# ScalarE's copies of the shared products: earlier places in its queue in the hybrid mLSTM / forgetting-attention / conformer layer

## The chip, the cores and the metric

One core of one Trainium2 chip runs the whole layer. The metric is the time of one execution on the device in microseconds (us); the times shown of the kernel before are the median of three runs.

## The reference

One transformer-like layer on 256 tokens of width 2048, followed by a last RMS norm. A wide input projection feeds three mixers (chunkwise mLSTM, forgetting attention, a conformer convolution), their outputs are projected back, and a squared-ReLU feed-forward network closes the layer. The change lies in the feed-forward network, in its second product:

```python
x = x + jnp.concatenate([y_m, y_a, y_c], axis=-1) @ w_out
h2 = rmsnorm(x, norm_ffn)
x = x + jnp.square(jax.nn.relu(h2 @ w_up)) @ w_down     # w_up 2048 x 8192, w_down 8192 x 2048
...
return rmsnorm(x, final_norm)
```

## The kernel before

**Arithmetic.** All matrix products are float32 in effect: each operand is split into a high part (`hi`, rounded to TensorE's fast float32 format) and a low part (`lo`, the rest), and three matmuls add hi·hi, hi·lo and lo·hi into one PSUM bank. Weights come through eight `raw` tiles of 512 KB (SyncE issues the loads, `load`, L351). For every half unit of weights (a step) ScalarE copies `raw` into `hi` (L442, or L410 in a seven-product step) and VectorE subtracts to get `lo` (L463 or L414). There are five `hi` and five `lo` buffers, so the split of step i+5 waits for TensorE to leave step i.

**The feed-forward network** runs in four quarters q = 0 to 3 of 2048 hidden columns. A quarter first makes four up blocks (kind B: 8 steps, four banks each, named f = 0 to 3 here), each squared and split into `hid`. Then `w_down` is applied in two pairs p = 0, 1 of output blocks of 512 columns (kind A: two banks each, one for each half of the tokens). There are four PSUM banks under the tag `mm` and four under `mx`. Tags t0 and t1 change places from quarter to quarter.

**Seven products in place of eight.** In a pair some chunks of four contraction tiles are multiplied by Strassen's scheme in Winograd's form. `SEVEN` gives the order of its seven steps:

```python
SEVEN = (("p3", 0, 1), ("p1", 1, 0), ("p2", 1, 1), ("p5", 1, 0), ("p7", 0, 0), ("p6", 0, 1), ("p4", 1, 1))
```

p2, p3 and p4 belong to one output each and add straight into the pair's own banks. p1, p5, p6 and p7 are shared by several outputs; they get the four banks of the other tag, t1, and must be copied out by ScalarE when the last seven-product chunk has added to them. `add_up` makes these four copies, chained in the order p1, p5, p6, p7 (though TensorE finishes p7 before p6): in q = 0 straight into an accumulator (L1381, tile `acc0`, or `fnb` for p = 1), in later quarters into a tile `zz` (L1386), two copies to a tile, and VectorE adds each tile to the accumulator (L1390). VectorE's four further steps (L1404 to L1417) bring the sums into the result once, after q = 2 for p = 1 and after q = 3 for p = 0 (`fin`). A seven-product step whose weights are sums of weights needs one more VectorE step, `raw<-raw` (L398), ahead of its `hi`. The plain blocks of `w_down` leave their banks by `gather` (ScalarE L1432 into `z`, VectorE L1438 into `x2t`).

**Where the four banks are wanted at once.** In pair p = 1 the units run y0 x0 s1 x3 s2 y3 (s: seven products, x and y: plain chunks of the two outputs). After p4, the last step of s2, TensorE has only y3 left (two steps, 24 matmuls) and then begins the next quarter's first up block, which takes the four t1 banks: f = 0 to 3 each wait for a copy. These are boundary 1 (q = 0 to 1, copies L1381), boundary 2 (q = 1 to 2) and boundary 3 (q = 2 to 3). In q = 3 the pair p = 0 runs x0 y0 x1 s2 y1 s3, and directly after p4 of s3 the plain block of column group 2 begins in the same tag, which takes two of the banks at once: boundary 4. The pairs p = 0 of q = 0 to 2 are followed by seven products of p = 1 only some steps later.

**What sets the order.** The program's text is written out by a planner while the kernel is built. Each engine has a queue of tasks with a cost, predecessors and a priority; when an engine is free by the planner's clock, it takes, of the tasks that are ready by then, the one with the lowest `prio`. `lag` is added to the time at which a task counts as ready. Splits of weights have prio -1, `gather`'s copies -2 with lag 0.3, the copies of shared products -0.8 with lag 1.5:

```python
r = max(r, d.fin + (0.0 if d.eng == t.eng else LAT))
q = room(t.takes)
return None if q is None else max(r + t.lag, q)
...
p = t.prio + (1.5 if t.table and t.table != table[0] else 0.0)
key = (0, p, i, r) if r <= now + 0.02 else (1, r, p, i)
```

On the chip each engine then works its list in that fixed order, and waits at each instruction for its semaphores.

Of the kernel before, what the change touches and what calls it, by code (L numbers as in the profile page):

```python
# [33 lines left out]
def trunk(ctx: ExitStack, tc, x, norm_mix, w_in, b_in, mlstm_conv_w, mlstm_conv_b,  # L34
# [3 lines left out]
    x, w_in, w_out, w_up, w_down, out = x[0], w_in[0], w_out[0], w_up[0], w_down[0], out[0]  # L38
# [9 lines left out]
    def sbt(pl, shape, name, dt=F32, bufs=1, tag=None):  # L48
        return pl.tile(shape, dt, name=name, tag=tag or name, bufs=bufs)
# [38 lines left out]
    def task(*a, **kw):  # L88
        t = Task(*a, **kw)
        queue[t.eng].append(t)  # L90
        return t

    def t_act(cost, fn, *a, **kw):
        return task("act", cost, fn, *a, **kw)

    def t_dve(cost, fn, *a, **kw):
        return task("dve", cost, fn, *a, **kw)

    def t_pe(cost, fn, *a, **kw):
        return task("pe", cost, fn, *a, **kw)  # L100
# [89 lines left out]
    def cd(n):  # L190
        return 0.13 + 0.00105 * n

    def cut(c):
        return slice(c * 512, (c + 1) * 512)
# [11 lines left out]
    def pl(name):  # L206
        return pools[name][1]
# [386 lines left out]
    wb = Buf(mm_rot)  # L594
# [24 lines left out]
    for j in range(2):  # L619
# [9 lines left out]
        for h in range(4):  # L629
            o = xt[j][:, cut(h)]  # L630
# [16 lines left out]
    for c2 in range(KC // 2):  # L647
        b = mx_buf()
        ts = []
# [121 lines left out]
    for i in range(2):  # L771
# [19 lines left out]
        for c in range(2):  # L791
            jg.append(join(lambda c=c, o_g=o_g: o_g(c), bg, c, col("bug", 4 + 2 * i + c),
                           takes=[gbuf] if c == 0 else [], deps=[jg[-1]]))
# [20 lines left out]
    for j in range(2):  # L814
# [16 lines left out]
        p = t_pe(0.45, f1, list(tap.values()), prio=20, takes=[b])  # L831
# [8 lines left out]
    for h in range(2):  # L840
# [22 lines left out]
        p = t_pe(0.45, f1, ln_t, prio=20, takes=[b], uses=[lnx_buf[0]])  # L863
# [3 lines left out]
        for c in range(2):  # L867
# [7 lines left out]
                  prio=-2, uses=[b.bufs[j]]) for j in range(2)]  # L875
# [334 lines left out]
    def seven_of(b0, b1, tag, stat, q):  # L1210
        return dict(b=(b0, b1), tag=tag, hid=stat, q=q,
                    extra={x: Buf(mx_rot if tag == "mx" else mm_rot) for x in SHARED},
                    done={x: Task("pe", 0.0, None) for x in SHARED})
# [114 lines left out]
    for c in range(4):  # L1328
# [6 lines left out]
        for i2 in range(2):  # L1335
# [10 lines left out]
            p = t_pe(0.45, f, ad, prio=-1, takes=[tb])  # L1346
# [23 lines left out]
    def add_up(p, q, o, fin):  # L1370

        ts, both = [late_open], []
        for m, x in enumerate(("p1", "p5", "p6", "p7")):
            if q and m % 2 == 0:
                wb = Buf(zz_rot)

            def f(m=m, x=x):
                if (p, 0) not in acc:
                    acc[p, 0] = sbt(pl("late"), [P, 4, 512], "acc0") if p == 0 else \
                        sbt(pl("late"), [P, D], "fnb").rearrange("p (m n) -> p m n", m=4)  # L1380
                act.activation(acc[p, 0][:, m, :], o["extra"][x].t, AF.Copy)  # L1381

            def f1(m=m, x=x, wb=wb if q else None):
                if m % 2 == 0:
                    wb.t = sbt(pl("late"), [P, 4, S], "zz", bufs=2).rearrange("p (m h) t -> p m (h t)", m=2)
                act.activation(wb.t[:, m % 2, :], o["extra"][x].t, AF.Copy)  # L1386

            def f2(m=m, wb=wb if q else None):
                t = acc[p, 0][:, m - 1:m + 1, :]
                dve.tensor_add(t, t, wb.t)  # L1390

            ts.append(t_act(0.6, f1 if q else f, [o["done"][x]] + ts[-1:], prio=-0.8,
                            takes=[wb] if q and m % 2 == 0 else [], uses=[o["extra"][x]], lag=1.5))
            if q and m % 2:
                both.append(t_dve(1.22, f2, [ts[-1]] + both, prio=-0.6, uses=[wb]))
        ts += both
        if not fin:
            return []

        def g(i):  # L1400
            a1, a5, a6, a7 = (acc[p, 0][:, m, :] for m in range(4))

            def out(j, c, t):
                dve.scalar_tensor_tensor(x2[0][:, j, cut(c)], t, rs2[:, j:j + 1], x2[0][:, j, cut(c)],  # L1404
                                         op0=OP.mult, op1=OP.add)

            if i == 0:
                dve.tensor_add(a6, a6, a1)
                out(0, 2 * p, a1)
            elif i == 1:  # L1410
                dve.tensor_add(a7, a7, a6)
                out(1, 2 * p, a7)
            elif i == 2:
                dve.tensor_add(a6, a6, a5)
                out(0, 2 * p + 1, a6)
            else:
                dve.tensor_add(a5, a5, a7)  # L1417
                out(1, 2 * p + 1, a5)

        gs = [ts[-1]]  # L1420
        for i in range(4):
            gs.append(t_dve(2 * cd(512), lambda i=i: g(i), [gs[-1], rs_t], prio=-0.5))
        return gs[1:]
# [17 lines left out]
    def x2_ap(j, sl):  # L1441
        return lambda: x2[0][:, j, sl]
# [4 lines left out]
    for q in range(4):  # L1447
        t0, t1 = (("mm", "mx"), ("mx", "mm"))[q % 2]
        for c in range(4):
            b = block_units(blk("B", 512, lambda: big["h"], "h", (t0, t1)[c % 2]), w_up, 2048 * q + 512 * c)  # L1450
            zb, wb = Buf(z_rot), Buf(zz_rot)
# [31 lines left out]
        for p in range(2):  # L1483
            sv = GROUPS[q, p]
            if not sv:
                for c in (2, 3):
                    bs[c] = block_units(down(c, t1), w_down, 512 * c, KC * q)
                continue
            b0, b1 = bs[2 * p], bs[2 * p + 1] = down(2 * p, t0), down(2 * p + 1, t0)
            o = seven_of(b0, b1, t1, lambda: big["hid"], "hid%d" % q)  # L1490
            pair_units(b0, b1, w_down, 1024 * p, KC * q, sv, p == 1,
                       lambda c: dict(o=o, sums=lambda: xsum[c], packed=packed(q, c), fourth=own if c == 3 else None))
            got = add_up(p, q, o, q == (3, 2)[p])
            for i, t in enumerate(got):
                shared[2 * p + i // 2, i % 2] = t
            if p == 1 and got:
                fn_t = t_ctl(fn_in, got)
# [22 lines left out]
    for j in range(2):  # L1520
# [8 lines left out]
        for h in range(2):  # L1529
            hs = slice(1536 + h * 256, 1792 + h * 256)  # L1530
            o = x2_ap(j, hs)
# [39 lines left out]
    for i, toks in items:  # L1571
        u, half = steps[i]["u"], steps[i]["h"]
        d = units[u]
        if steps[i]["p"]:
            p, o, g = steps[i]["p"], steps[i]["o"], steps[i]["g"]
# [30 lines left out]
        m = len(d["ks"]) // 2  # L1606
# [68 lines left out]
```

## Time and profile before

| | us |
|---|---|
| median of three runs (1135.47 to 1137.18) | 1135.47 |
| the profiled execution | 1134.14 |
| its span | 1131.7 |
| TensorE busy in the span | 1111.2 (98%) |
| VectorE busy | 874.0 (77%) |
| ScalarE busy | 655.6 (58%) |

The time of the profiled execution is its span and 2.4 us around it. Busy time is a sum over the whole span; where a change in one place counts, the rows of that place say what each engine waited for. A row of the timeline has the start, the duration, the engine, the line, the operation and its tiles (out<-in), the count of instructions merged into it, and in brackets the idle time ahead of it with what ended it. The durations of matmuls are modelled (0.39), while their starts are recorded: in an unbroken stream the starts lie 0.227 apart.

### The profile page before, as it was taken

To read this page: it belongs to the slowest core of one execution; us is meant where nothing else is said; L and a number is where in the kernel's file an instruction comes from. 1 tells how busy PE (TensorE), PEld (TensorE's weight loads), DVE (VectorE), ACT (ScalarE), POOL (GpSimd) and SP (SyncE) were. 2 spreads that over 40 slices of the span, in tenths; PEclk is the share of its full clock that TensorE was granted. 3 is DMA by queue.
4 is the path that set the end of the run, shared out by engine and by line. 5 is a ranking of instruction groups with operands and counts; after the bars stand their busy time and mean duration, and the time that the engine had idled before them with its cause. 6 is when DMAs were issued, how large, how long until landed. Compare 5 with 4: busy or idle time off the path is not lost.

```text
span 1131.7 us, 15579 instructions
## 1 busy us (share of the span) xinstructions
PE 1111.2 (98%) x5812; PEld 950.7 (84%) x5812; DVE 874.0 (77%) x1160; ACT 655.6 (58%) x932; POOL 17.0 (2%) x40
## 2 busy tenths in 40 slices
PE   8999999999999999999999999999999999999996
PEld 7888788888888888888887888887888887888875
DVE  6679998887676786668994677996577999567993
ACT  7445376777775565545664554765454666455662
POOL 1000000010000000000000000000000000000000
PEclk9999999999999999999999999999999999999998
DMA  8866554547555385565756555657644658655452
GB/s 308 254 196 193 185 167 137 181 149 242 168 183 167 121 269 169 154 202 164 228 192 235 168 169 161 232 183 243 190 163 149 225 186 270 225 173 186 160 175 74
DMA packets 130818, 214.97 MB, mean 190 GB/s; under 512 B 6796, under 2 KB 48056, under 8 KB 130360
## 3 DMA queue, kind: packets, MB, share of 16 engines
q1 hardware_dynamic: 130136, 212.93, 58.2%
q10 hardware_dynamic: 608, 1.06, 0.3%
q8 instruction: 45, 0.74, 0.3%
q14 instruction: 29, 0.24, 0.1%
HBM read 211.87 MB, written 2.10 MB: 189 GB/s over the span
## 4 chain that ended last, share of the span: by engine, by line
PE 94%; DMA 2%; ACT 1%; issue 1%; DVE 1%; POOLq 0%; POOL 0%; ACTq 0%; DVEq 0%
PE mm L57 64%; PE mx L57 30%; DMA raw<-in_w_in_dram 1%; DMA x<-in_x_dram 1%; ACT hi L442 0%; DMA rowp<-in_norm_mix_dram 0%; ACT z L1432 0%; ACT zz L1386 0%; PE mx L1343 0%; PE mx L989 0%; DMA rowp<-in_norm_ffn_dram 0%; DVE lo L414 0%; DVE lo L463 0%; ACT x2t L1548 0%; PE mx L1022 0%
## 5 line engine op out<-in xcount | busy, mean ns | idle before, releaser
L463 DVE TENSOR_TENSOR lo<-raw,hi 128x1024 fp32r<-128x1024 f32 x332 | 397.7, 1223 | 192.6 <-issue 129.3
L442 ACT ACTIVATE hi<-raw 128x1024 fp32r<-128x1024 f32 x332 | 346.5, 1057 | 263.9 <-PE mm L57 166.7
L410 ACT ACTIVATE hi<-raw 128x1024 fp32r<-128x1024 f32 x105 | 111.5, 1062 | 93.2 <-PE mm L57 34.9
L57 PE MATMUL mm<-hi,hid 128*128 128x512 f32 x488 | 155.3, 389 | 2.2 <-ACT zz L1386 2.2
L57 PE MATMUL mm<-x,hi 128*128 128x512 f32 x640 | 156.4, 394 | 0.0
L414 DVE TENSOR_TENSOR lo<-raw,hi 128x1024 fp32r<-128x1024 f32 x105 | 126.5, 1223 | 13.1 <-ACT hi L410 12.5
L57 PEld LDWEIGHTS mm<-x,hi 128*128 128x128 f32 x640 | 116.9, 188 | 23.1 <-ACT tmp L564 0.4
L57 PE MATMUL mx<-h,hi 128*128 128x512 f32 x512 | 123.0, 391 | 3.9 <-ACT fnb L1381 2.3
L57 PE MATMUL mm<-h,hi 128*128 128x512 f32 x512 | 123.2, 391 | 1.7 <-ACT zz L1386 1.5
L57 PEld LDWEIGHTS mx<-h,hi 128*128 128x128 f32 x512 | 94.1, 188 | 23.3 <-ACT fnb L1381 3.1
L57 PEld LDWEIGHTS mm<-h,hi 128*128 128x128 f32 x512 | 94.0, 188 | 21.0 <-ACT zz L1386 2.0
L57 PEld LDWEIGHTS mm<-hi,hid 128*128 128x128 f32 x488 | 91.6, 188 | 21.6 <-ACT zz L1386 2.7
L57 PE MATMUL mx<-hi,hid 128*128 128x512 f32 x304 | 98.5, 389 | 0.0
L57 PE MATMUL mm<-lo,hid 128*128 128x512 f32 x244 | 95.1, 390 | 0.1
L57 PEld LDWEIGHTS mm<-x,lo 128*128 128x128 f32 x640 | 82.0, 191 | 3.2
L57 PE MATMUL mm<-x,lo 128*128 128x256 f32 x640 | 83.0, 282 | 0.0
L398 DVE TENSOR_TENSOR raw<-raw 128x1024 f32<-128x1024 f32 x60 | 73.3, 1222 | 0.7
L57 PE MATMUL mm<-hi,y 128*128 128x512 f32 x232 | 73.5, 392 | 0.0
L57 PEld LDWEIGHTS mm<-h,lo 128*128 128x128 f32 x512 | 65.6, 191 | 2.5
L57 PEld LDWEIGHTS mx<-h,lo 128*128 128x128 f32 x512 | 65.7, 191 | 2.5
L57 PEld LDWEIGHTS mx<-hi,hid 128*128 128x128 f32 x304 | 57.1, 188 | 11.8
L57 PE MATMUL mm<-h,lo 128*128 128x256 f32 x512 | 66.4, 283 | 0.0
(244 smaller groups left out, 1289.5 us busy)
## 6 DMA issues: line engine op xcount, KB each, us to landing
raw<-in_w_up_dram SPq DMA_DIRECT2D x128, 512.0 KB, 3.8
raw<-in_w_down_dram SPq DMA_DIRECT2D x128, 512.0 KB, 5.1
raw<-in_w_in_dram SPq DMA_DIRECT2D x92, 512.0 KB, 3.5
raw<-in_w_out_dram SPq DMA_DIRECT2D x32, 512.0 KB, 4.6
raw<-in_w_in_dram SPq DMA_DIRECT2D x8, 516.0 KB, 3.4
raw<-in_w_in_dram SPq DMA_DIRECT2D x4, 544.0 KB
x<-in_x_dram SPq DMA_DIRECT2D x8, 256.0 KB, 4.2
x2t<-in_x_dram SPq DMA_DIRECT2D x2, 1024.0 KB
```

What stands on the lines that cost most here:

```text
L57: pe.matmul(o, l, r, start=start, stop=stop, skip_group_check=True)
L398: sums[i] = t_dve(C_LO, lambda: dve.tensor_sub(piece(*o), piece(*l), piece(*r)), after + [arrival(*l), arrival(*r)], prio=-1)
L410: act.activation(hl[i][0], piece(u, h), AF.Copy)
L414: dve.tensor_sub(hl[i][1], piece(u, h), hl[i][0].bitcast(F32))
L442: act.activation(hl[i][0], raws[u, h][0], AF.Copy)
L463: dve.tensor_sub(hl[i][1], raws[u, h][0], hl[i][0].bitcast(F32))
```

## The change

`add_up` gets a flag `soon`, true for p = 1 in every quarter and for the pair that is closed (`fin`). Where it is true the copies of shared products get prio -2 in place of -0.8 and lag 0.3 in place of 1.5. Elsewhere nothing changes.

```diff
     def add_up(p, q, o, fin):
 
         ts, both = [late_open], []
+        soon = p == 1 or fin
         for m, x in enumerate(("p1", "p5", "p6", "p7")):
...
-            ts.append(t_act(0.6, f1 if q else f, [o["done"][x]] + ts[-1:], prio=-0.8,
-                            takes=[wb] if q and m % 2 == 0 else [], uses=[o["extra"][x]], lag=1.5))
+            ts.append(t_act(0.6, f1 if q else f, [o["done"][x]] + ts[-1:], prio=-2 if soon else -0.8,
+                            takes=[wb] if q and m % 2 == 0 else [], uses=[o["extra"][x]], lag=0.3 if soon else 1.5))
```

No instruction is added or removed; TensorE's order is the same. The lists of ScalarE and VectorE change around the four boundaries. Lines behind the new one have numbers higher by one.

ScalarE at boundary 1, before, from the copy of p1 (the L1381 are p1, p5, p6, p7; L410 is the high part of p4; the first two L442 those of y3, then the next up block's):

```order
L1381 ACTIVATE fnb<-mx 128x512
L1432 ACTIVATE z<-mm,st 128x512
L410 ACTIVATE hi<-raw 128x1024
L442 ACTIVATE hi<-raw 128x1024 x4
L1432 ACTIVATE z<-mm,st 128x512
L442 ACTIVATE hi<-raw 128x1024 x2
L1381 ACTIVATE fnb<-mx 128x512
L442 ACTIVATE hi<-raw 128x1024
L1432 ACTIVATE z<-mm,st 128x512
L1381 ACTIVATE fnb<-mx 128x512
L1432 ACTIVATE z<-mm,st 128x512
L1381 ACTIVATE fnb<-mx 128x512
```

and now:

```order
L1382 ACTIVATE fnb<-mx 128x512
L1433 ACTIVATE z<-mm,st 128x512
L1382 ACTIVATE fnb<-mx 128x512
L410 ACTIVATE hi<-raw 128x1024
L442 ACTIVATE hi<-raw 128x1024
L1382 ACTIVATE fnb<-mx 128x512
L442 ACTIVATE hi<-raw 128x1024
L1382 ACTIVATE fnb<-mx 128x512
L1433 ACTIVATE z<-mm,st 128x512
L442 ACTIVATE hi<-raw 128x1024 x5
```

The copy of p5 stands ahead of p4's high part, that of p6 behind y3's first high part and that of p7 behind its second; before, three of them stood behind seven or more high parts.

ScalarE at boundary 2, before, from the copy of p1 (the L1386 are p1, p5, p6, p7); boundary 3 reads the same with `mm` and `mx` exchanged:

```order
L1386 ACTIVATE zz<-mm 128x512
L1432 ACTIVATE z<-mx,st 128x512
L1386 ACTIVATE zz<-mm 128x512
L410 ACTIVATE hi<-raw 128x1024
L442 ACTIVATE hi<-raw 128x1024 x4
L1432 ACTIVATE z<-mx,st 128x512
L442 ACTIVATE hi<-raw 128x1024 x2
L1386 ACTIVATE zz<-mm 128x512
L442 ACTIVATE hi<-raw 128x1024
L1432 ACTIVATE z<-mx,st 128x512
L1386 ACTIVATE zz<-mm 128x512
```

and now:

```order
L1387 ACTIVATE zz<-mm 128x512
L1433 ACTIVATE z<-mx,st 128x512
L1387 ACTIVATE zz<-mm 128x512
L410 ACTIVATE hi<-raw 128x1024
L1387 ACTIVATE zz<-mm 128x512
L442 ACTIVATE hi<-raw 128x1024
L1387 ACTIVATE zz<-mm 128x512
L442 ACTIVATE hi<-raw 128x1024
L1433 ACTIVATE z<-mx,st 128x512
L442 ACTIVATE hi<-raw 128x1024 x5
L1433 ACTIVATE z<-mx,st 128x512
```

The copies of p1 and p5 keep their places. The copy of p6 now stands ahead of both high parts of y3, and that of p7 between them.

VectorE at boundary 2, before, from the add of p1 and p5 (L1390; L414 is the low part of p4, then come y3's two and the next block's):

```order
L1390 TENSOR_TENSOR fnb<-fnb,zz 128x1024
L414 TENSOR_TENSOR lo<-raw,hi 128x1024
L463 TENSOR_TENSOR lo<-raw,hi 128x1024 x6
L1438 TENSOR_TENSOR x2t<-x2t,z 128x2x512
L463 TENSOR_TENSOR lo<-raw,hi 128x1024
L1390 TENSOR_TENSOR fnb<-fnb,zz 128x1024
L1438 TENSOR_TENSOR x2t<-x2t,z 128x2x512
```

and now:

```order
L1391 TENSOR_TENSOR fnb<-fnb,zz 128x1024
L414 TENSOR_TENSOR lo<-raw,hi 128x1024
L463 TENSOR_TENSOR lo<-raw,hi 128x1024
L1391 TENSOR_TENSOR fnb<-fnb,zz 128x1024
L463 TENSOR_TENSOR lo<-raw,hi 128x1024 x6
L1439 TENSOR_TENSOR x2t<-x2t,z 128x2x512 x2
```

The add of p6 and p7 has moved from the end of this piece to between the two low parts of y3.

ScalarE at boundary 4, before, around the copy of p1 (the first L1386; L410 is the high part of p4, the L442 are those of the plain block that follows):

```order
L1432 ACTIVATE z<-mx,st 128x512
L1386 ACTIVATE zz<-mm 128x512
L1432 ACTIVATE z<-mx,st 128x512
L410 ACTIVATE hi<-raw 128x1024
L442 ACTIVATE hi<-raw 128x1024 x4
L1432 ACTIVATE z<-mx,st 128x512
L442 ACTIVATE hi<-raw 128x1024
L1386 ACTIVATE zz<-mm 128x512 x2
L442 ACTIVATE hi<-raw 128x1024
L1386 ACTIVATE zz<-mm 128x512
```

and now:

```order
L1387 ACTIVATE zz<-mm 128x512
L1433 ACTIVATE z<-mx,st 128x512 x2
L1387 ACTIVATE zz<-mm 128x512
L410 ACTIVATE hi<-raw 128x1024
L442 ACTIVATE hi<-raw 128x1024
L1387 ACTIVATE zz<-mm 128x512
L442 ACTIVATE hi<-raw 128x1024
L1387 ACTIVATE zz<-mm 128x512
L442 ACTIVATE hi<-raw 128x1024 x2
L1433 ACTIVATE z<-mx,st 128x512
```

The copy of p5 stands ahead of p4's high part, those of p6 and p7 behind the first and second high part of the block that follows.

VectorE at boundary 4, before, from the sum of weights (L398) that p4 needs:

```order
L398 TENSOR_TENSOR raw<-raw 128x1024
L1438 TENSOR_TENSOR x2t<-x2t,z 128x2x512
L414 TENSOR_TENSOR lo<-raw,hi 128x1024
L463 TENSOR_TENSOR lo<-raw,hi 128x1024 x5
L1438 TENSOR_TENSOR x2t<-x2t,z 128x2x512
L1390 TENSOR_TENSOR acc_5417<-acc_5417,zz 128x1024
```

and now:

```order
L398 TENSOR_TENSOR raw<-raw 128x1024
L1439 TENSOR_TENSOR x2t<-x2t,z 128x2x512
L1391 TENSOR_TENSOR acc_5417<-acc_5417,zz 128x1024
L414 TENSOR_TENSOR lo<-raw,hi 128x1024
L463 TENSOR_TENSOR lo<-raw,hi 128x1024 x6
L1439 TENSOR_TENSOR x2t<-x2t,z 128x2x512
```

The add of p1 and p5 into the accumulator now stands ahead of p4's low part (L414).

## Rows read from the trace of the kernel before

**Rows 1.** The page's first part: busy us, share of the span, instructions.

```profile
PE 1111.2 (98%) x5812; PEld 950.7 (84%) x5812; DVE 874.0 (77%) x1160; ACT 655.6 (58%) x932; POOL 17.0 (2%) x40
```

**Rows 2.** TensorE's waits, 429 to 1120 us: total us, times, longest.

```profile
PE mm L57 <- ACT zz L1386: 3.8, 2, 2.2
PE mx L57 <- ACT fnb L1381: 2.3, 2, 1.8
PE mx L57 <- ACT zz L1386: 1.5, 1, 1.5
```

**Rows 3.** The timeline around boundary 1.

```profile
588.13 0.39 PE L57 MATMUL mx<-hi,xsums 128*128 128x512 f32 x1
...
588.29 1.06 ACT L410 ACTIVATE hi<-raw 128x1024 fp32r<-128x1024 f32 x1 [0.40 <-DVE raw L398]
...
589.38 1.23 DVE L414 TENSOR_TENSOR lo<-raw,hi 128x1024 fp32r<-128x1024 f32 x1 [1.19 <-ACT hi L410]
...
591.08 0.39 PE L57 MATMUL mm<-hi,hid 128*128 128x512 f32 x1
...
597.88 0.61 PE L57 MATMUL mx<-h,hi 128*128 128x512 f32 x2
...
600.65 0.61 ACT L1381 ACTIVATE fnb<-mx 128x512 f32<-128x512 f32 x1
...
601.31 3.28 PE L57 MATMUL mx<-h,hi 128*128 128x512 f32 x13 [0.56 <-ACT fnb L1381]
```

**Rows 4.** The timeline around boundary 2.

```profile
761.73 0.39 PE L57 MATMUL mm<-hi,xsums 128*128 128x512 f32 x1
...
762.15 0.60 ACT L1386 ACTIVATE zz<-mm 128x512 f32<-128x512 f32 x1 [0.67 <-PE mm L57]
...
762.67 1.06 ACT L410 ACTIVATE hi<-raw 128x1024 fp32r<-128x1024 f32 x1
...
763.64 3.89 ACT L442 ACTIVATE hi<-raw 128x1024 fp32r<-128x1024 f32 x4
...
764.45 0.39 PE L57 MATMUL mm<-hi,xsums 128*128 128x512 f32 x1
...
765.06 6.90 DVE L463 TENSOR_TENSOR lo<-raw,hi 128x1024 fp32r<-128x1024 f32 x6
...
766.24 0.62 PE L57 MATMUL mx<-hi,hid 128*128 128x512 f32 x2
766.70 0.39 PE L57 MATMUL mx<-lo,hid 128*128 128x512 f32 x1
...
771.91 0.84 PE L57 MATMUL mm<-h,hi 128*128 128x512 f32 x3
...
773.65 0.59 ACT L1386 ACTIVATE zz<-mm 128x512 f32<-128x512 f32 x1
...
774.29 1.89 PE L57 MATMUL mm<-h,hi 128*128 128x512 f32 x7 [1.53 <-ACT zz L1386]
```

**Rows 5.** The timeline around boundary 4.

```profile
1072.27 0.39 PE L57 MATMUL mm<-hi,xsums 128*128 128x512 f32 x1
...
1072.57 1.22 DVE L1438 TENSOR_TENSOR x2t<-x2t,z 128x1024 f32<-128x1024 f32 x1
...
1073.84 1.23 DVE L414 TENSOR_TENSOR lo<-raw,hi 128x1024 fp32r<-128x1024 f32 x1
...
1075.22 0.39 PE L57 MATMUL mx<-hi,hid 128*128 128x512 f32 x1
...
1077.03 0.39 PE L57 MATMUL mm<-hi,hid 128*128 128x512 f32 x1
...
1079.02 1.07 ACT L1386 ACTIVATE zz<-mm 128x512 f32<-128x512 f32 x2
1079.65 0.50 PE L57 MATMUL mm<-hi,hid 128*128 128x512 f32 x1 [2.23 <-ACT zz L1386]
```

**Rows 6.** ScalarE's longest sum of waits, 429 to 1120 us, same columns.

```profile
ACT hi L442 <- PE mm L57: 85.8, 56, 2.7
```

## The prediction

> **What bounds the kernel.** I read the busy times first: TensorE 98%, VectorE 77%, ScalarE 58% of the span [rows 1]. So time is to be won only where TensorE stands still, and I read its list of waits over the feed-forward network next. It holds three lines with five waits, 7.6 us together, and all end with a copy of a shared product [rows 2]; no transfer and no weight split stands in it. Then I read the timeline around each boundary, since idle time there is counted from modelled ends; I count from starts, of which an unbroken stream has one every 0.227 us.
>
> At boundary 1 the new block starts its bank 0 and bank 1 at 597.88, could start bank 3 at 597.88 + 3 x 0.227 = 598.56, and starts it at 601.31, behind the copy of p7 at 600.65 [rows 3]: 2.75 us lost. At boundary 2 bank 0 starts at 771.91, bank 3 could at 772.59 and does at 774.29, again behind p7's copy at 773.65 [rows 4]: 1.70 us. Boundary 3 has the same order and shows the same idle time (1.5 us in both, the mx line and the rest of the mm line [rows 2]): 1.70 us. At boundary 4 the second bank could start at 1077.03 + 0.23 = 1077.26 and does at 1079.65, behind the copies at 1079.02 [rows 5]: 2.39 us. Together **8.54 us**, which is all that there is to win.
>
> **The waits that go.** In the new lists all four copies stand ahead of at most one or two weight splits of what follows p4. At boundary 2 p7's copy can run at about 766.4 (worked out below) where bank 3 is wanted at 772.6; at boundary 1 at about 592.8, wanted at 598.6; at boundary 4 p5's copy at 1072.7, wanted at 1077.3. So I take all of the 8.54 us as removed. No instruction is added, so nothing else is charged but the places: what stands behind a copy that waits.
>
> **The waits that come.** ScalarE's new list has copies that wait for TensorE, and behind them stand the high parts, behind those VectorE's low parts, and for these TensorE waits. Some durations: a copy starts 0.42 after the start of the product's last matmul (761.73 to 762.15), the next instruction 0.52 later (762.67), a high part takes 1.06, a low part 1.23 with one every 1.15 (6.90 for six), both read off boundary 2 [rows 4].
>
> *Boundaries 2 and 3.* p6's last matmul starts at 764.45, so its copy cannot start before 764.87. ScalarE is free at 763.64, when before it began y3's first high part [rows 4]. It now idles 1.23, copies, and begins that high part at 765.39, ready at 766.45; VectorE's low part follows from 766.49 and is ready for TensorE, with 0.04 for the signal, at 767.75. TensorE wants the high part at 766.47 and the low part, its second matmul, at 766.70 [rows 4]. The high part is just in time, the low part 1.05 late. Next comes p7's copy (766.36), y3's second high part (766.9 to 767.9), VectorE's add of p6 and p7 (767.6 to 768.9) and the second low part, 768.8 to 770.0; TensorE, now 1.05 later, wants it near 770.5: just in time, by 0.5. Net at each of the two: 1.70 - 1.05 = **0.65**.
>
> *Boundary 1.* Here the copy of p5 has moved ahead of p4's high part. p5's last matmul starts at 588.13, its copy at 588.55, the high part at 589.07 in place of 588.29: 0.78 later. The low part then starts at 590.16 in place of 589.38 and is ready at 590.16 + 1.23 + 0.04 = 591.43; TensorE wants it at 591.08 + 0.23 = 591.31 [rows 3]: 0.12 late. y3's first high part now stands ahead of p6's copy and is ready at 591.1; its low part at 592.6, wanted at 592.8. Net 2.75 - 0.12 = **2.63**.
>
> *Boundary 4.* p5's last matmul starts at 1072.27, its copy at 1072.69, p4's high part at 1073.21, ready at 1074.27. But VectorE now adds p1 and p5 between the add at 1072.57 and p4's low part, which therefore moves from 1073.84 by one add to about 1074.85 and is ready at 1076.12; TensorE wants it at 1075.22 + 0.23 = 1075.45 [rows 5]: 0.67 late. The low part behind it is ready at 1077.25, wanted at 1077.6. Net 2.39 - 0.67 = **1.72**.
>
> Sum: 2.63 + 0.65 + 0.65 + 1.72 = 5.65. TensorE works on alone behind every boundary and the last block ends the span, so I take the gain through to the end one for one. VectorE's closing steps behind q = 2 and q = 3 change places with low parts that are made five steps ahead; I cost that at nothing. If that cover were gone, a low part late by one add would cost up to 1.2. The final norm's load moves back by two weight loads in SyncE's queue; it is wanted only near the end of q = 3, and two loads come ahead of it instead of behind: nothing again.
>
> [...] ScalarE idled 0.67 ahead of p5's copy at 762.15 and the high part behind it began only at 762.67, after the copy [rows 4]. [...]
>
> **The sum against the times.** The profiled execution took 1134.14, of which 1131.7 is span; it would take 1134.14 - 5.65 = 1128.5. The median of the three runs is 1.33 above the profiled one, so the forecast for the median is 1135.47 - 5.65 = **1129.8 us**. About 0.2% (2.3 us) is what a measurement of this kernel can tell from no change.
>
> **Bounds of the terms.** What goes is measured; the new waits are worked out from chained durations, and each link can be off by one slot. From below they are nothing: 8.54 gained, 1126.9. From above: at boundary 1 a low part is late by another 1.15, one slot of VectorE, at boundaries 2 and 3 the second low part of y3 is late too (0.5 of margin against one slot of 1.15: 0.65 more each), at boundary 4 one slot more: 1.15 + 0.65 + 0.65 + 1.15 = 3.6 less, that is 2.05 gained, 1133.4. I take the chain as worked out, since each of its links is a distance that this stretch itself shows.
>
> **Rivals.**
>
> *All of it is won: 1126.9.* For it: high parts run up to four in a row ahead of TensorE (763.64, four in 3.89 [rows 4]), and ScalarE's largest sum of waits is high parts that wait for TensorE to leave a buffer, 85.8 us in 56 waits [rows 6], so in most places a high part has time in hand. Against it: just here y3's low part, made from 765.06 to 766.28, has only 0.38 in hand, and the copy of p6 costs its high part 1.75.
>
> *It is given back: about 1134.5, no change that can be told.* The removed idle time of TensorE comes back as waits for splits behind the boundary: buffers come free earlier, and ScalarE and VectorE, which before caught up while TensorE stood, do not. For it: at boundary 2 the add of p6 and p7 has also moved ahead of y3's second low part. Against it: VectorE has 23% and ScalarE 42% of the span free [rows 1], so a lag of 1.4 us is made up in some 6 us of VectorE's time, while the block's low parts are made several steps ahead. With one further low part late by a whole slot at each boundary the gain is 5.65 - 4 x 1.15 = 1.05.
>
> *Slower: about 1140.* One mechanism: the copies at the head of ScalarE's queue hold the high parts, and the lag reaches TensorE in full. Price at its worst, at each boundary: the wait for p6 (1.23), two copies ahead of the high part (2 x 0.52) and one add ahead of the low part (1.15), 3.4 us; four times 13.7 against 8.54 gained, 5.1 slower, 1140.6. It decides where the first low part behind the copies comes later by more than the time in hand and the old wait together: at boundary 2 by more than 0.38 + 1.70 = 2.08 us. I work out a shift of 766.49 - 765.06 = 1.43 there, 0.78 at boundary 1 and 1.0 at boundary 4, all short of that, and at boundary 4 against 0.34 + 2.39. So this needs a wait that I have not seen.
>
> *The change does not do what it says.* It could fail only if the new order were another than written; the lists show the moves at all four boundaries, so I give it nothing of its own.
>
> **How the numbers follow.** Forecast (gain of 4 to 7): 0.71. All won: 0.09. Given back: 0.13, of which a third still gains over 0.2%. Slower: 0.07. Faster by over 0.2%: 0.71 + 0.09 + 0.04 = 0.84; within 0.2%: 0.10; slower by over 0.2%: 0.06, the last rival but for its small end. The range takes the bounds of the terms, 1126.9 and 1133.4, and leaves the given-back and slower cases out, 0.16 to 0.2 together: 1126.9 to 1133.4.
>
> **What would show it.** In the trace after, TensorE's waits on lines of the copies (L1382, L1387) should be gone or under 0.3 us each. In their place there should be a gap of some 1 us ahead of the second matmul of y3 at boundaries 2 and 3, ended by the low part L463, one of 0.1 to 0.2 at boundary 1 and one of 0.6 to 0.7 ahead of p4's second matmul at boundary 4, both ended by L414. ScalarE should idle some 1.2 us ahead of p6's copy at boundaries 2 and 3. Each quarter's first up block should start unbroken over all four banks. If TensorE still waits at bank 3, the copies come later than worked out; if no gap stands ahead of y3, the first rival holds; if gaps turn up two or more steps behind a boundary, the gain is being given back.

## The result and the profile after

| | before | after |
|---|---|---|
| median | 1135.51 us (1135.19 to 1137.18, 6 runs) | 1127.99 us (1127.71 to 1128.21, 6 runs) |
| ratio, 95% interval | | 0.9932 [0.9919, 0.9945] |
| span of the profiled execution | 1131.7 us | 1125.8 us |

The change makes the kernel 0.7% faster, 7.5 us in the median and 5.9 us between the two profiled spans. Both numbers count: over all runs on record, those of before lie in groups, near 1133.8, 1135.5 and 1137 us, and its profiled execution (1134.14) is one of the lowest; runs of after all lie within 0.5 us.

Busy times on the page of after, to set beside [rows 1]:

```profile
PE 1110.5 (99%) x5812; PEld 950.2 (84%) x5812; DVE 873.7 (78%) x1160; ACT 655.8 (58%) x932; POOL 17.0 (2%) x40
```

TensorE's waits of after, 429 to 1120 us (total us, times, longest), against [rows 2]:

```profile
PE mm L57 <- DVE lo L463: 0.8, 1, 0.8
PE mx L57 <- DVE lo L463: 0.8, 1, 0.8
PE mx L57 <- DVE lo L414: 0.5, 1, 0.5
```

All five waits for copies are gone. Three shorter ones for low parts, 2.1 us together, have come: the L463 at boundaries 2 and 3, the L414 at boundary 4.

The timeline of after at boundary 1, against [rows 3]:

```profile
588.41 0.60 ACT L1382 ACTIVATE fnb<-mx 128x512 f32<-128x512 f32 x1 [0.67 <-PE mx L57]
588.90 1.05 ACT L410 ACTIVATE hi<-raw 128x1024 fp32r<-128x1024 f32 x1
...
589.99 1.23 DVE L414 TENSOR_TENSOR lo<-raw,hi 128x1024 fp32r<-128x1024 f32 x1 [1.94 <-ACT hi L410]
...
591.27 0.50 PE L57 MATMUL mm<-lo,hid 128*128 128x512 f32 x1
591.61 0.64 PE L57 MATMUL mm<-hi,hid 128*128 128x512 f32 x2
...
598.01 3.79 PE L57 MATMUL mx<-h,hi 128*128 128x512 f32 x16
```

The copy of p5 (588.41) is first and p4's high part follows. The low part is done so that its matmul starts at 591.27, 0.11 behind the 591.16 that an unbroken stream would have had. The new block's sixteen first matmuls run as one piece from 598.01, over all four banks.

At boundary 2, against [rows 4]:

```profile
762.08 0.60 ACT L1387 ACTIVATE zz<-mm 128x512 f32<-128x512 f32 x1 [1.14 <-PE mm L57]
762.57 1.05 ACT L442 ACTIVATE hi<-raw 128x1024 fp32r<-128x1024 f32 x1
763.45 0.74 PE L57 MATMUL mx<-hi,hid 128*128 128x512 f32 x2
...
763.66 1.22 DVE L463 TENSOR_TENSOR lo<-raw,hi 128x1024 fp32r<-128x1024 f32 x1 [1.30 <-ACT hi L442]
...
764.94 0.50 PE L57 MATMUL mx<-lo,hid 128*128 128x512 f32 x1 [0.75 <-DVE lo L463]
...
770.28 3.79 PE L57 MATMUL mm<-h,hi 128*128 128x512 f32 x16
```

Here the lines show the whole price: ScalarE stands 1.14 us ahead of p6's copy, y3's high part begins only behind it at 762.57, VectorE's low part at 763.66, and the matmul that needs it starts at 764.94 in place of 763.91, 1.03 late. The block behind (770.28) is again unbroken.

At boundary 4, against [rows 5]:

```profile
1069.54 1.22 DVE L1391 TENSOR_TENSOR acc<-acc,zz 128x1024 f32<-128x1024 f32 x1
...
1070.67 1.22 DVE L414 TENSOR_TENSOR lo<-raw,hi 128x1024 fp32r<-128x1024 f32 x1
...
1071.05 0.39 PE L57 MATMUL mx<-hi,hid 128*128 128x512 f32 x1
...
1071.95 0.50 PE L57 MATMUL mx<-lo,hid 128*128 128x512 f32 x1 [0.50 <-DVE lo L414]
```

The add of p1 and p5 stands ahead of p4's low part. Its matmul is wanted at 1071.28 and starts at 1071.95, 0.67 late.

I counted all of TensorE's lateness at the four boundaries in this manner, from one recorded start to the next and against 0.227 us a matmul: before 2.92 + 2.24 + 2.27 + 2.51 = 9.94 us, after 0.23 + 1.55 + 1.55 + 0.79 = 4.12 us. The difference, 5.82, is the 5.9 us between the spans. What it leaves out is the rest of the median's 7.5.

### The profile page after: what moved, and what is told of

Its sections match the earlier page's. It is cut to its first block, busy times and chain, and to the rows that moved or that the text cites. A ratio compares the mean times of both kernels' runs of the same rounds, so it can differ in the third digit from the quotient of the medians.

```text
span 1125.8 us, 15581 instructions
## 1 busy us (share of the span) xinstructions
PE 1110.5 (99%) x5812; PEld 950.2 (84%) x5812; DVE 873.7 (78%) x1160; ACT 655.8 (58%) x932; POOL 17.0 (2%) x40
## 4 chain that ended last, share of the span: by engine, by line
PE 96%; DVE 1%; DMA 1%; issue 1%; ACT 1%; POOLq 0%; POOL 0%; ACTq 0%; DVEq 0%
PE mm L57 65%; PE mx L57 30%; DMA x<-in_x_dram 1%; ACT hi L442 0%; DMA rowp<-in_norm_mix_dram 0%; PE mx L989 0%; PE mx L1343 0%; DVE lo L463 0%; DVE lo L414 0%; PE mx L656 0%; ACT x2t L1549 0%; PE mx L1022 0%; DVE x L642 0%; DVE h L642 0%; DVE x L635 0%
## 5 line engine op out<-in xcount | busy, mean ns | idle before, releaser
L463 DVE TENSOR_TENSOR lo<-raw,hi 128x1024 fp32r<-128x1024 f32 x332 | 397.7, 1222 | 185.9 <-issue 124.4
L442 ACT ACTIVATE hi<-raw 128x1024 fp32r<-128x1024 f32 x332 | 346.7, 1058 | 255.0 <-PE mm L57 160.0
L410 ACT ACTIVATE hi<-raw 128x1024 fp32r<-128x1024 f32 x105 | 111.5, 1062 | 91.9 <-PE mm L57 34.4
L414 DVE TENSOR_TENSOR lo<-raw,hi 128x1024 fp32r<-128x1024 f32 x105 | 126.3, 1221 | 13.8 <-ACT hi L410 12.9
L398 DVE TENSOR_TENSOR raw<-raw 128x1024 f32<-128x1024 f32 x60 | 73.2, 1220 | 0.7
L57 PE MATMUL mx<-h,lo 128*128 128x256 f32 x512 | 66.4, 283 | 0.0
```

What stands on the lines that cost most here:

```text
L57: pe.matmul(o, l, r, start=start, stop=stop, skip_group_check=True)
L398: sums[i] = t_dve(C_LO, lambda: dve.tensor_sub(piece(*o), piece(*l), piece(*r)), after + [arrival(*l), arrival(*r)], prio=-1)
L410: act.activation(hl[i][0], piece(u, h), AF.Copy)
L414: dve.tensor_sub(hl[i][1], piece(u, h), hl[i][0].bitcast(F32))
L442: act.activation(hl[i][0], raws[u, h][0], AF.Copy)
L463: dve.tensor_sub(hl[i][1], raws[u, h][0], hl[i][0].bitcast(F32))
```

## Experiments

The edits are shown against the changed kernel, where nothing else is said.

**The boundaries apart.** Three kernels make the change at one kind of boundary only, and a fourth is the kernel before again, on the same chip.

```diff
-        soon = p == 1 or fin
+        soon = p == 1 and q == 0        # boundary 1 only
```

> The change at boundary 1 alone. Theory of the chain of slots (the prediction's sum): 2.63 us gained, 1132.9 by the median. Rival that all the old wait is won: 2.75. Rival that something besides the four boundaries went (the medians moved by 7.5 us where the sum has 5.65): the part in which it lies gains 1.4 to 1.9 us more than its term; here 4 to 4.5 if it lies at boundary 1.

```diff
-        soon = p == 1 or fin
+        soon = p == 1 and q > 0         # boundaries 2 and 3 only
```

> The change at boundaries 2 and 3 alone. Theory of the chain: 2 x 0.65 = 1.3 us gained, 1134.2, a gap of 1.04 us ahead of the second matmul of y3 at each. All of the old wait won: 3.4 us. Extra beyond the boundaries lying here: 2.7 to 3.2.

```diff
-        soon = p == 1 or fin
+        soon = p == 0 and fin           # boundary 4 only
```

> The change at boundary 4 alone. Theory of the chain: 2.39 - 0.67 = 1.72 us gained, 1133.8. All won: 2.39. Extra lying here: 3.1 to 3.6.

> The kernel before, unchanged, for a second trace of it. If its profiled execution in the first trace was a short one, the span here is 1 to 1.4 us over 1131.7, and the rows show where: at a boundary (then the terms of the sum are larger than the first trace had them) or elsewhere (then the change took it away in passing). If not, the span is 1131.7 and the time 1134.1.

| change at | median, us | lowest | ratio [95%] | gain, medians | gain, lowest runs | term predicted |
|---|---|---|---|---|---|---|
| none (before again) | 1135.55 | 1133.42 | 0.9997 [0.9987, 1.0007] | 0.1 | | |
| boundary 1 | 1132.42 | 1131.12 | 0.997 [0.996, 0.998] | 3.2 | 2.7 | 2.63 |
| boundaries 2 and 3 | 1133.99 | 1132.60 | 0.9986 [0.9977, 0.9995] | 1.7 | 1.2 | 1.30 |
| boundary 4 | 1133.50 | 1132.20 | 0.9975 [0.9966, 0.9985] | 2.2 | 1.6 | 1.72 |

The medians are set against 1135.65 (29 runs of before shared by the four, 1133.80 to 1138.16), the lowest runs against 1133.80. By lowest runs the three gains are near the predicted terms, and together 5.5; a lowest run is known only to some 0.4 us, as before again went down to 1133.42 on the same chip. The starts in the traces are firmer: before less after they give 2.69 at boundary 1, 0.69 and 0.72 at 2 and 3, and 1.72 at 4. By medians the three gains make 7.0, near the whole 7.5. They are 0.4 to 0.6 over the term at every one of the three, where the expectations had looked for the whole extra in one place. So nothing is missing between the boundaries; what is missing is something that the middle run of before has and its lowest does not.

The second trace of before was taken to catch it, but its execution was one of the lowest again (1133.42, span 1131.0), so no trace of before itself shows a longer run. The trace of the kernel with boundary 1 alone does, since its profiled execution (1132.66) was not one of the lowest. Behind boundary 4, which this kernel leaves as it was, TensorE waits 2.2 us for a copy, and then:

```profile
1076.69 0.79 PE L57 MATMUL mm<-hi,hid 128*128 128x512 f32 x1 [2.23 <-ACT zz L1387]
1077.28 0.63 PE L57 MATMUL mm<-lo,hid 128*128 128x512 f32 x1
1077.70 1.05 PE L57 MATMUL mm<-hi,hid 128*128 128x512 f32 x2
1078.56 0.63 PE L57 MATMUL mm<-lo,hid 128*128 128x512 f32 x1
1078.98 1.02 PE L57 MATMUL mm<-hi,hid 128*128 128x512 f32 x2
1079.84 0.39 PE L57 MATMUL mm<-lo,hid 128*128 128x512 f32 x1
```

The starts are 0.42 us apart (1077.28 to 1077.70) where they are 0.227 elsewhere. The windows of the same kernel (stretch; us; for PE, PEld, DVE, ACT and POOL busy us and count; granted clock; DMA share; GB/s):

```profile
1074.00:1076.00 2.00, 0.46 (x3) 0.03 (x1) 2.00 (x3) 2.00 (x3) 0.00 (x0) 1.00 0.97 280
1076.00:1078.00 2.00, 1.31 (x3) 1.12 (x4) 2.00 (x3) 1.12 (x3) 0.00 (x0) 0.60 0.64 166
1078.00:1080.00 2.00, 2.00 (x6) 1.52 (x6) 2.00 (x2) 0.00 (x0) 0.00 (x0) 0.54 0.99 366
1080.00:1082.00 2.00, 2.00 (x11) 1.61 (x10) 0.45 (x2) 1.50 (x2) 0.00 (x0) 1.00 1.03 379
```

Behind the wait the granted clock falls to 0.60 and 0.54, the means of two windows of 2 us, and is back at 1.00 from 1080 on. From 1076.69 to 1079.84 seven matmuls take 3.15 us in place of 7 x 0.227 = 1.59; some 0.1 of that is the first spacing behind the waits at the boundaries, 0.34 at full clock too (below), so the fall costs **about 1.45 us**. The other two kernels, whose boundary 1 is as before, show a clock of 0.83 there in 600 to 610 us, behind the two waits for copies; counted in the same way they lose 1.6 each. The profiled execution of before has 1.00 throughout 600 to 770 and 1060 to 1080. Shown here are the first of the two waits at boundary 1 in the trace of before (the second is the last of [rows 3]), then TensorE's windows of before and of the kernel with boundaries 2 and 3 alone (stretch; us; busy us and count; granted clock; DMA share; GB/s):

```profile
600.25 0.50 PE L57 MATMUL mx<-h,hi 128*128 128x512 f32 x1 [1.76 <-ACT fnb L1381]
```

```profile
600.00:610.00 10.00, 9.19 (x46) 1.00 0.60 216
600.00:610.00 10.00, 9.43 (x42) 0.83 0.45 151
```

The distances between the groups of runs, 1133.8, 1135.5 and 1137, are about that price: no fall, one, two. The mean granted clock, on record for 65 runs of before, goes with the groups: 0.997 or 0.998 in the ten lowest (1133.35 to 1134.28), 0.996 or 0.997 in the 38 of the middle (1135.12 to 1135.97), 0.995 in all 16 above (1136.61 to 1137.41), 0.993 in the one at 1138.16.

**The waits filled.** If the clock is the cause, then the kernel before with its waits kept, but TensorE kept at work in them, must lose the upper groups of runs. The edit is on the kernel before: 18 transposes of the identity into bank 0 of the new block, ahead of its first matmul, at boundaries 1 and 4. What they write is overwritten when the block starts.

```diff
+            fill[b] = 18 if q == 1 and c == 0 else 0
...
+                    fill[bs[c]] = 18 if c == 2 else 0
...
+            for _ in range(fill.get(b, 0)):
+                pe.transpose(b.bufs[0].t[:, 0:P], ident, ident)
```

> The kernel before with 18 transposes of the identity ahead of the first matmul at boundary 1 and at boundary 4, each 18 x 0.116 = 2.1 us: TensorE works where it stood still, and the wait for the last copy ends when it did (bank 3 at 601.31, second bank at 1079.65). Theory that part of the time went with a fall of the granted clock behind the two long waits (seen at 1076 to 1080 us in b1_only and at 600 to 610 in b23_only and b4_only): no fall behind either boundary, the runs lie together near the shortest of the kernel before, 1133.8, some 1.8 us under its median of 1135.65. Theory that all of the 7.5 us are the waits themselves, larger than the trace had them: 1135.6, unchanged. If the transposes push the blocks back: slower by up to 1 us.

Measured: 1133.92 us (1133.51 to 1134.04, 10 runs) beside 1135.61 (1133.83 to 1137.41, 19 runs) for the kernel without them, 0.9984 [0.9975, 0.9994]. Work was added, no work was removed, no copy comes earlier, and the kernel is 1.7 us faster. Its timeline at boundary 1, then windows of TensorE alone behind boundaries 1 and 4 (stretch; us; busy us and count; granted clock; DMA share; GB/s):

```profile
597.66 2.12 PE L1626 MATMUL mx<-ident 128*128 128x128 f32 x18
599.54 0.99 PE L57 MATMUL mx<-h,hi 128*128 128x512 f32 x3
601.10 3.26 PE L57 MATMUL mx<-h,hi 128*128 128x512 f32 x13 [0.56 <-ACT fnb L1381]
```

```profile
600.00:610.00 10.00, 9.44 (x51) 1.00 0.61 211
1070.00:1080.00 10.00, 9.77 (x52) 1.00 0.83 241
```

The last bank is begun at 601.10 (601.31 in [rows 3]), so the wait as such is there still; the clock stays at 1.00 (the ten runs have means of 0.997 or 0.998), and the upper groups of runs are gone. The waits of 1.5 us at boundaries 2 and 3 are not filled and brought none of the ten runs above 1134.04.

**The place of p6's copy.** At boundaries 2 and 3 the copies of p6 and p7 are moved back by their lag so that p6's follows y3's first high part (a lag of 1.1, where the expectation names 1.5; the order in the trace is the one that it describes), and then the other way, ahead of p4's high part (lag -1).

```diff
-  lag=0.3 if soon else 1.5
+  lag=(1.1 if q in (1, 2) and x in ('p6', 'p7') else 0.3) if soon else 1.5
```

> The changed kernel, but at boundaries 2 and 3 the copies of p6 and p7 have lag 1.5, so that p6's stands behind y3's first high part and p7's behind the two after it. Theory of the chain: y3's low part is no longer late, 1.04 us more at each of the two, 2.1 us under the changed kernel: 1125.9. Rival that the gap ahead of y3's second matmul comes from VectorE's add or a transfer and not from the copy of p6 ahead of the high part: 1128.0.

Measured: 1125.94 us (1125.78 to 1126.08, 4 runs), 0.9914 [0.9899, 0.9929]; 2.1 less than after, the two waits of 1.03. ScalarE at boundary 2 begins y3's first high part at 760.94, ahead of p6's copy; in the trace of after it began behind the copy, at 762.57:

```profile
760.94 1.04 ACT L442 ACTIVATE hi<-raw 128x1024 fp32r<-128x1024 f32 x1
762.18 0.60 ACT L1387 ACTIVATE zz<-mm 128x512 f32<-128x512 f32 x1 [0.20 <-PE mm L57]
```

TensorE's waits are one line:

```profile
PE mx L57 <- DVE lo L414: 0.5, 1, 0.5
```

```diff
-  lag=0.3 if soon else 1.5
+  lag=(-1.0 if q in (1, 2) and x in ('p6', 'p7') else 0.3) if soon else 1.5
```

> The changed kernel, but at boundaries 2 and 3 the copies of p5, p6 and p7 all stand ahead of p4's high part (lag -1 for p6 and p7). Theory of the chain: p6's copy at 764.87 and p7's at 765.36 by the old clock, p4's high part from 765.9 to 766.9, its low part behind VectorE's second add, 767.1 to 768.4; TensorE's second matmul of p4 is 3.2 us late against 1.70 won, 1.5 lost at each boundary against the kernel before and 2.15 against the changed one: 1128.0 + 4.3 = 1132.3, plus 1.3 to 1.5 for each fall of the clock if the longer wait brings one. Rival that ScalarE's place in the order costs nothing as long as the copies are early: 1128.0 or less.

Measured: 1136.61 us (1132.28 to 1137.58, 10 runs), 1.0002 [0.999, 1.0013]. TensorE's longest waits, and its windows behind them (same columns):

```profile
PE mx L57 <- ACT hi L410: 2.1, 1, 2.1
PE mm L57 <- ACT hi L410: 2.1, 1, 2.1
```

```profile
760.00:770.00 10.00, 7.14 (x21) 0.71 0.59 192
764.20:770.90 6.70, 5.96 (x14) 0.50 0.64 216
935.00:945.00 10.00, 6.93 (x24) 0.83 0.56 185
```

Without a fall of the clock the expectation was 1132.3, and the lowest run is 1132.28. But TensorE now waits over 2 us at boundaries 2 and 3, for a high part and not for a bank, the clock falls behind both, and eight of the ten runs lie 4 to 5 us higher. The expectation had put each fall at 1.3 to 1.5; here each costs more, since the lower clock lasts nearly 7 us (0.50 from 764.20 to 770.90) in place of some 3 (1076.69 to 1079.84 above). Counted from starts as above it is 2.6 us at boundary 2 and 2.9 at boundary 3, 5.4 together, and the profiled run (1137.58) lies 5.3 above the lowest. Put too early, the copies eat all that the change gains. In the changed kernel and in this one a high part stands behind a copy that is not ready, and TensorE pays: 1.03 us at each of the two boundaries in the changed kernel, a wait of 2.1 at each for the high part itself in this one.

**The two halves of the change.** Priority alone, and lag alone.

```diff
-  prio=-2 if soon else -0.8, ... lag=0.3 if soon else 1.5
+  prio=-2 if soon else -0.8, ... lag=1.5
```

> The new priority alone, lag 1.5 as before. The order: at boundary 1 p5's copy behind p4's high part, at 2 and 3 p6's behind y3's first high part, at 4 p5's behind p4's high part and VectorE's add behind p4's low part. Theory of the chain: 2.75 + 1.70 + 1.70 won in full, at boundary 4 the first low part of the next block 0.6 late, 1.8 net: 7.95 of waits and 1.8 of clock against the kernel before, 1125.8. Rival that copies must come as early as the change puts them: 1128.0 or over.

```diff
-  prio=-2 if soon else -0.8, ... lag=0.3 if soon else 1.5
+  prio=-0.8, ... lag=0.3 if soon else 1.5
```

> The new lag alone, priority -0.8 as before. The order: p5's copy early, those of p6 and p7 together behind seven high parts but ahead of the last one that waits for TensorE to end y3 (770.4 and 770.9 by the old clock, bank 3 wanted at 772.6); at boundary 4 as the changed kernel. Theory of the chain: 2.63 + 1.70 + 1.70 + 1.72 = 7.75 of waits, no long wait left and so 1.8 of clock: 1126.0. Rival that the priority carries the gain: near 1135.6.

Measured: priority alone 1125.22 us (1125.04 to 1125.51, 4 runs), 0.9912 [0.9899, 0.9926]; lag alone 1125.77 us (1125.44 to 1125.91, 4 runs), 0.9916 [0.9901, 0.9932]. Both are a little under what was expected (by 0.6 and 0.2), and each half does more than both together, 1128.0. The idea that the priority carries the gain and the lag does nothing (1135.6) has fallen. With either alone, y3's high part at boundary 2 begins ahead of p6's copy (760.26 and 760.82; 762.57, behind it, with both), and neither trace has a wait there; what remains for priority alone is the first, for lag alone the second of these lines:

```profile
PE mm L57 <- DVE lo L463: 0.4, 1, 0.4
```

```profile
PE mx L57 <- DVE lo L414: 0.5, 1, 0.5
```

**The adds later too.** Priority alone, and VectorE's adds of the copied pairs counted as ready 2 us later at boundaries 2, 3 and 4 (boundary 1 has no such add), so that they don't stand ahead of a low part.

```diff
-  lag=0.3 if soon else 1.5
+  lag=1.5
...
-                both.append(t_dve(1.22, f2, [ts[-1]] + both, prio=-0.6, uses=[wb]))
+                both.append(t_dve(1.22, f2, [ts[-1]] + both, prio=-0.6, uses=[wb], lag=2.0 if soon else 0.0))
```

> The new priority with lag 1.5, and VectorE's add of two copies gets lag 2 where soon is set, so that at every boundary p4's low part stands ahead of the add. Theory of the chain: nothing late at any boundary, also not the 0.30 that p4's low part was late at boundaries 2 and 3 in the kernel before: 8.5 + 0.3 of waits and 1.8 of clock, 1124.9. If the adds moved into the last block cost the end of the kernel: 1125.5 to 1126.5.

Measured: 1124.10 us (1123.94 to 1124.44, 4 runs), 0.9903 [0.9889, 0.9916], the fastest of all and 0.8 under what was expected. The view of TensorE's waits has no line left between 429 and 1120 us. Counted from starts, the lateness at the four boundaries is 0.49 us, against 4.12 after the change: 3.6 less, and the spans differ by 1125.8 - 1122.2 = 3.6.

**The changed kernel again**, beside these:

> The changed kernel, unchanged, beside the three others on one chip: 1128.0, its runs within 0.5 us of each other since no wait is left behind which the clock fell, the kernel before at 1133.8, 1135.5 and 1137 in groups.

Measured: 1128.07 us (1127.89 to 1128.24, 5 runs), 0.9937 [0.9925, 0.995], span 1125.6.

## Why the prediction was right, and which term it lacked

*The waits that go* went: all five of [rows 2], and no wait for a copy is left. *The waits that come* came where they were worked out, with the predicted engine and line behind each:

| boundary | new wait predicted | measured | net predicted | net by starts, before less after |
|---|---|---|---|---|
| 1 | 0.12 | 0.11 | 2.63 | 2.69 |
| 2, 3 | 1.05 each | 1.03 each | 1.30 together | 1.41 together |
| 4 | 0.67 | 0.67 | 1.72 | 1.72 |

ScalarE's idle time ahead of p6's copy, predicted as 1.23, is 1.14. The chain of slots, each link a distance that the same stretch shows, held to 0.1 us. The steps costed at nothing (VectorE's closing steps, the moved load) cost nothing that a trace shows: the lateness at the boundaries accounts for the spans. The lower bound of the new waits, nothing, and the upper, one slot more at each place, were both far from what came.

*The step that was mis-sized is the sum against the times.* The prediction took 5.65 from the profiled execution and the same 5.65 from the median, and called 8.54 us of waits "all that there is to win". The profiled execution moved by 5.9, but the median by 7.5. The missing 1.8 us is the clock: behind the long waits at boundaries 1 (1.76 and 0.56 with one matmul between) and 4 (2.23), which the change removes, most executions of before (55 of the 65 above, by their granted clock and the groups of their times) run some 3 us at a lower clock, at 1.45 to 1.6 us a time, and the profiled one did not; the fall itself stands in the traces of the kernels with one kind of boundary changed (0.60 and 0.54 in two windows of 2 us, 0.83 in one of 10). The row that could have told it was the spread of the three runs shown, 1135.47 to 1137.18 above a profiled 1134.14: two separate values for one program. The word "all" fell as well: the best version gains 1135.5 - 1124.1 = 11.4, since the waits counted at the last bank only were not the whole lateness (9.94 by starts), and the clock comes on top. That 1127.99 lies inside the range owes something to luck: the range was made for the new waits alone, and without these the same clock would have brought some 1125, below it.

*The rivals.* "All of it is won" did not hold, for the reason given against it: the low part of y3 had only 0.38 in hand. The time after, 1127.99, does come near its 1126.9, but the traces show the clock as the cause and not the missing new waits. "It is given back" fell: no wait two steps or more behind a boundary. "Slower" did not hold for this change, but its mechanism is real. It was to decide at a shift of more than 2.08 us at boundary 2; with the copies first the wait ahead of p4 is 2.1 and more follows, and that kernel is back at the time of before.

*The order of ScalarE's list.* The terms of 0.65 at boundaries 2 and 3 rest on y3's high part waiting behind p6's copy. The experiments on the place of that copy show that it does: the high part begins at 762.57 behind the copy and at 760.94 with the copy put behind it, and 2.1 us come back (1128.0 to 1125.9). The idle time of 0.67 ahead of p5's copy, which the prediction sets beside the high part that began at 762.67, could not show it: p4's high part needs the sum of weights that VectorE makes in L398, and in the trace of before this ended only at 762.58:

```profile
761.36 1.22 DVE L398 TENSOR_TENSOR raw<-raw 128x1024 f32<-128x1024 f32 x1
```

*What stays open.* Why the clock falls in one execution of before and not in the next, with the same waits, no run settles. Between the waits of 1.5 us (ten runs without a fall) and those of 1.76 with 0.56 behind (falls) nothing was measured. No wait was filled at one of boundaries 1 and 4 alone; but with only the long wait at 4 left (boundary 1 changed) the one trace has a fall behind 4 and five of eight runs lie some 0.7 us or more over the lowest three; with only that at 1 left (boundary 4 changed) the trace has a fall behind 1 and seven of ten runs do. So each brings falls by itself.

## What to carry to other kernels

Cost a reordering by walking each queue link by link between starts that the stretch itself shows; that gave each new wait here to 0.1 us. Here a copy that frees a bank had a best place: behind the split that is needed next, ahead of the ones that have time in hand; at boundaries 2 and 3 either half of this change avoids holding that split (1125.2 and 1125.8 us), and both together put the copy too early (1128.0). Where runs of one kernel fall into groups, compare the clock behind its long waits in executions of different groups before taking one profile as the kernel's time: here a wait of about 2 us, where the clock fell behind it, cost another 1.45 to 1.6, and up to 2.9 in one kernel.

## What the runs showed of the hardware

- A wait of TensorE of 2.2 us (or of 1.76 and 0.56 close together) in an otherwise full stream was followed in most, not all, executions (55 of 65 of before, by the groups of their times) by some 3 us at a lower clock (granted 0.54 to 0.60 in the windows over it, starts 0.42 apart), a loss of 1.45 to 1.6 us; with 18 small transposes ahead of each of the two places no run of ten lay above 1134.04 and the windows there show 1.00.
- Where a wait of 2.1 us had another of 0.7 to 1.0 one matmul behind it (the copies put first), the lower clock lasted nearly 7 us (granted 0.50 from 764.20 to 770.90) and cost 2.6 and 2.9 us.
- Behind the waits at the boundaries the first spacing of matmuls is longer at full clock too: 591.27 to 591.61 in after, 0.34 in place of 0.227, so by starts each new wait costs 0.11 more than its length.
- ScalarE did not begin a high part while a copy ahead of it in its list waited: behind p6's copy y3's first high part began at 762.57, with the copy put behind it at 760.94 (p6_behind), and the kernel went from 1128.0 to 1125.9 us.
